# Weight parts of the first up unit made early and kept in DRAM, residual work in halves between the w_ple blocks, sums of squares on VectorE

## The chip, the cores and the metric

The kernel runs on one core of a Trainium2 chip. The metric is the device time of the whole launch in microseconds. Before the change three runs took 2024.33 to 2029.08 us, median 2027.07.

## The reference

One layer of a streaming encoder on 1056 tokens (1024 of a prompt, 32 of a sample), width 1024, all in float32. The attention and recurrence branches are mixed to `mix`; what matters here starts there:

```python
x = x + _rms_norm(mix @ w_out, g_post_mix)          # x1

hf = _rms_norm(x, g_pre_ffn)
a, u = jnp.split(hf @ w_up, 2, axis=-1)             # w_up: 1024 x 5632
...
ffn = (jax.nn.gelu(ac, approximate=True) * u) @ w_down
x = x + _rms_norm(ffn, g_post_ffn)
...
x = x + (pe @ w_ple) * jax.nn.sigmoid(x @ w_ple_gate)   # w_ple: 256 x 1024
```

## The kernel before

Activations lie with features on partitions and tokens on the free axis. From w_out on, the tokens stand in four groups of 264 (`H`), two to a pair. Every float32 product is made of three matmuls on float32r parts: a value is cast to a high part on ScalarE (`S.copy`, L182 and L1424 for weights, L1366 for activations) and the low part is the difference, made on VectorE (L185, L1425, L1367). `product` issues high x high, high x low and low x high (L201 to L203). A weight column block is loaded by SP into one of two `wr` buffers, and its two parts take two of eight `wb` buffers; `next_w` keeps the parts of two further blocks ahead.

The stages around the change, in the order of the program:

- **out**, two pairs (loop over `p`), each over eight columns `c` of w_out: one block of 24 matmuls of 128x264 for each of the pair's two groups, into one of six PSUM banks `mm`. `z_out` scales the bank into `z[g]` and squares it on ScalarE (L1281, L1283, L1286) and adds the squares on VectorE (L1287).
- During pair 1, for groups 0 and 1: `pair_norm(0)` (sums over partitions by one-column matmuls against `ones`, L1307; a reciprocal root on VectorE, L1318 and L212 to L218; then row scales spread over partitions by small matmuls, L302, and copied to `rbT`, L304), `x1_part` (product with the row scale, L1335, addition of x, L1336, store to `x1_d` by POOL, L1337, gain on ScalarE, L1339), `x1_squares` (L1345 to L1352) for the second norm, and `build_ops(0)`, which makes from z the seven operands of a Strassen-like 2x2 product, each cast (L1366) and differenced (L1367), with five more subtractions and additions (L1370, L1371, L1374, L1378) between.
- **w_ple blocks**: `ple_product(g)` for four groups of eight blocks of 6 matmuls. ScalarE copies each bank to a tile `ple` (L1401; three tiles of four columns), POOL stores it (L1403). Between the groups stand, for groups 2 and 3: `pair_norm(1)`, `x1_part(2)`, `x1_part(3)`, and `build_ops(1)`.
- **up units**, 22 of them. A unit multiplies seven weight parts with seven operands (L1582 to L1584) into banks X, Y and Z (the same PSUM as the six `mm` banks). `unit_raw` loads the unit's 2 x 512 KB of w_up by SP (L1413); `unit_parts` makes the seven parts, with four additions between (L1431 to L1433, L1438); `prepare(n)` runs it three parts ahead of the use. Unit 0 runs pair 0 first and then pair 1, so that pair 1's operands have time to be made; `after` evicts the banks (L1593 to L1611), and a bank's next group waits for that. Later units run both pairs at once.
- In unit 0, `last_ops` squares x1 of groups 2 and 3 on VectorE (L1551) and takes the last steps of `build_ops(1)`; `x1_sums` sums each group's squares over features by 3 x 8 x 2 one-column matmuls, 48 trace rows a group (L1307), then `pair_norm` makes the second row scale.

The order of the instructions on each engine is set by the framework's scheduler from the program's order, except where `behind(engine)` pins what follows behind the last instruction of that engine. Each engine runs its own list in order, and so do SP and POOL with the transfers that they issue; a transfer whose wait isn't over holds those behind it.

```python
def behind(*engines):
    st = ExitStack()
    for e in engines:
        ins = next(i for i in reversed(nc.cur_bb.bb.instructions) if i.engine == e.engine)
        st.enter_context(tc.issue_after(ins))
    return st
```

Of the kernel before, what the change touches and what calls it, by code (L numbers as in the profile page):

```python
# [59 lines left out]
def layer_kernel(  # L60
# [65 lines left out]
    act_d = [dp.tile([P, T], F32, name=f"act_d{f}") for f in range(NF)]  # L126

# [1181 lines left out]
    def pair_norm(p, scale, t=None):  # L1309
# [15 lines left out]
        if sums:  # L1325
            rows()
        return rows

    def x1_part(g):

        rb = rbT[:, H * g:H * g + H]
        for i in range(2):
            zz = z[g][:, 4 * i:4 * i + 4, :].bitcast(F32)
            x = x1q[g][i]
            V.tensor_tensor(zz, zz, rb.unsqueeze(1).to_broadcast([P, 4, H]), op=ALU.mult)  # L1335
            V.tensor_tensor(x[:], x[:], zz, op=ALU.add)  # L1336
            gdma(x1_d[:, 4 * i:4 * i + 4, H * g:H * g + H], x[:])  # L1337
            for k in range(4):
                S.mul(z[g][:, 4 * i + k, :].bitcast(F32), x[:, k, :], g_ffn[:, 4 * i + k:4 * i + k + 1])  # L1339

    def x1_squares(g):

        for i in range(2):
# [6 lines left out]
            else:  # L1350
                V.tensor_tensor(x[:, 0, :], x[:, 0, :], x[:, 1, :], op=ALU.add)
                V.tensor_tensor(sqz[g][:], sqz[g][:], x[:, 0, :], op=ALU.add)  # L1352

# [39 lines left out]
    def ple_product(g):  # L1393
        xs = pT.pop(g)
        for c in range(8):
# [6 lines left out]
            if c % 4 == 3:  # L1402
                gdma(ple_d[:, c - 3:c + 1, H * g:H * g + H], t[:])  # L1403

# [11 lines left out]
    def unit_parts(u):  # L1416

        f1, f2 = raw_w.pop(u)
        s1 = wp.tile([P, 4, P], F32, tag="wb", name=nm("sa"), bufs=8)[:]
        a11, a12, a21, a22 = f1[:, 0:4, :], f1[:, 4:8, :], f2[:, 0:4, :], f2[:, 4:8, :]  # L1420

        def parts(src):
            t = wp.tile([P, 2, 4, P], F32R, tag="wb", name=nm("wt"), bufs=8)
            S.copy(t[:, 0], src)  # L1424
            V.tensor_tensor(t[:, 1], src, t[:, 0].bitcast(F32), op=ALU.subtract)  # L1425
            ready_w.append(t)
# [3 lines left out]
        parts(a11)  # L1430
# [4 lines left out]
        parts(a11)  # L1435
        yield
        parts(a12)
        adder.tensor_tensor(a12, a12, a11, op=ALU.add)  # L1438
        yield
        parts(a21)  # L1440
        yield
        parts(s1)
        yield
        parts(a22)
        yield
        parts(a12)
        yield

    AHEAD = 3
    n_parts, gens = [0], {}  # L1450

    def prepare(n):

        while n_parts[0] < min(n + 1, 7 * NF):
            u, i = divmod(n_parts[0], 7)
            if i == 0:
                if u not in raw_w:
                    unit_raw(u)
                gens[u] = unit_parts(u)
# [52 lines left out]
    next(op1)  # L1512
    next(op1)
    prepare(2)
    ple_product(3)

# [41 lines left out]

    def x1_sums(g):
        if g == 2:  # L1560
            x1_t.append(tr_bank())
        with behind(E):
            sums88(x1_t[0], g, [x1q[g][k // 4][:, k % 4, :] for k in range(KT)])

    def up_unit(u):
# [294 lines left out]
```

## Time and profile before

| | |
|---|---|
| three runs | 2029.08, 2027.07, 2024.33 us; median 2027.07 |
| the profiled execution | 2029.94 us, span from first to last instruction 2028.2 us |
| mean granted TensorE clock | 0.995 |
| busy share: PE, DVE, ACT, POOL | 99%, 71%, 47%, 11% |
| out, pair 0 / pair 1 | 1065.0 to 1111.4 / 1111.4 to 1163.9 us |
| w_ple blocks | 1163.9 to 1197.1 us |
| up unit 0 / unit 1 from | 1197.1 / 1236.2 us |

PE is TensorE's matmuls, PEld its weight loads, DVE is VectorE, ACT ScalarE, POOL GpSimd. Times in rows are us from the span's start unless marked ns. A row of the timeline has start, duration, engine, line, operation, tiles, count and, in brackets, how long the engine stood idle before it and what ended that. A row of a table by stretches has length, busy time (count of instructions) of each engine, the granted clock (1.00 is full), the busy share of the 16 DMA engines and GB/s. A row of grouped instructions has count, busy time, mean ns of one, idle time before them and what ended it. A DMA row has count, KB each and the median from issue to landing, where the trace has it. Some matmul records can be missing. Line numbers are those of the kernel before, except where a run's own are named.

### The profile page before, as it was taken

The page shows a single profiled execution, that of the slowest core. Times are in us where ns is not written, and L with a number is a line of the kernel's source. Part 1 is how long each engine was busy: PE and PEld are TensorE (multiplying, and loading weights), DVE is VectorE, ACT ScalarE, POOL GpSimd, SP SyncE. Part 2 cuts the span into 40 slices and gives each one's busy share as a digit, 9 for nine tenths or more (in the row PEclk, how much of TensorE's full clock was granted, in tenths as well). Part 3 has the DMA queues.
Part 4 walks back from the last instruction along what each step waited for, and adds up shares of the span by engine and source line. Part 5 has one row for each costly group of instructions (what it writes and reads, how often), then busy time and mean ns, then how long its engine had stood idle before and what let it go on. Part 6 is the DMA issues. An engine that isn't in the chain of part 4 may idle for free.

```text
span 2028.2 us, 37446 instructions
## 1 busy us (share of the span) xinstructions
PE 1999.8 (99%) x14366; PEld 1970.6 (97%) x14366; DVE 1441.1 (71%) x3194; ACT 960.0 (47%) x2177; POOL 219.3 (11%) x307
## 2 busy tenths in 40 slices
PE   8999999999999999999999989999999999999998
PEld 6999999999999999999999989999999999999998
DVE  6778788688888888553553877888888884655552
ACT  6555556556666666441224753333333343444432
POOL 2001110000000000002000112333333310000000
PEclk9999999999999999999999998999999999999999
DMA  8322321411111111486653561222222245655542
GB/s 255 104 64 93 103 74 53 154 42 57 57 46 47 44 46 53 138 250 204 204 152 108 159 200 53 86 74 85 74 82 77 79 144 193 219 179 181 165 128 83
DMA packets 247640, 233.79 MB, mean 115 GB/s; under 512 B 13013, under 2 KB 218344, under 8 KB 247461
## 3 DMA queue, kind: packets, MB, share of 16 engines
q1 hardware_dynamic: 240501, 209.15, 33.3%
q0 software_dynamic: 6880, 22.17, 3.1%
q8 instruction: 113, 1.85, 0.4%
q14 instruction: 66, 0.54, 0.1%
q10 hardware_dynamic: 80, 0.07, 0.0%
HBM read 171.79 MB, written 59.55 MB: 114 GB/s over the span
## 4 chain that ended last, share of the span: by engine, by line
PE 88%; DVE 6%; issue 2%; DMA 2%; ACT 1%; POOL 0%; SPq 0%; ACTq 0%; DVEq 0%; POOLq 0%
PE mm L201 13%; PE mm L202 13%; PE mm L203 13%; PE st L1584 7%; PE st L1583 7%; PE st L1582 7%; PE G L841 2%; PE Y L838 2%; PE G L840 2%; PE G L838 2%; PE Y L841 2%; PE Y L840 2%; PE tr L470 1%; PE X L838 1%; PE so L1032 1%
## 5 line engine op out<-in xcount | busy, mean ns | idle before, releaser
L1582 PE MATMUL st<-op,wt 128*128 128x264 f32 x1232 | 351.2, 285 | 2.5 <-ACT ple L1401 2.5
L1584 PE MATMUL st<-op,wt 128*128 128x264 f32 x1232 | 352.6, 286 | 0.0
L1583 PE MATMUL st<-op,wt 128*128 128x264 f32 x1232 | 350.5, 285 | 0.0
L185 DVE TENSOR_TENSOR wl<-wr,wh 128x1024 fp32r<-128x1024 f32 x134 | 164.1, 1224 | 144.9 <-ACT wh L182 137.8
L1582 PEld LDWEIGHTS st<-op,wt 128*128 128x128 f32 x1232 | 234.0, 190 | 2.8 <-ACT ple L1401 2.8
L1583 PEld LDWEIGHTS st<-op,wt 128*128 128x128 f32 x1232 | 234.1, 190 | 0.0
L1584 PEld LDWEIGHTS st<-op,wt 128*128 128x128 f32 x1232 | 233.6, 190 | 0.0
L182 ACT CAST wh<-wr 128x1024 fp32r<-128x1024 f32 x115 | 120.7, 1050 | 213.9 <-PE mm L202 161.3
L201 PE MATMUL mm<-ac,wh 128*128 128x352 f32 x528 | 171.0, 324 | 0.9 <-DVE Sp L1611 0.9
L1424 ACT CAST wt<-wu 128x512 fp32r<-128x512 f32 x132 | 81.4, 620 | 190.7 <-POOL ab L1568 93.3
L203 PE MATMUL mm<-ac,wl 128*128 128x352 f32 x528 | 169.9, 322 | 0.0
L202 PE MATMUL mm<-ac,wh 128*128 128x352 f32 x528 | 169.5, 321 | 0.0
L201 PE MATMUL mm<-La,wh 128*128 128x384 f32 (+1 forms) x504 | 166.9, 332 | 0.0
L202 PE MATMUL mm<-Lb,wh 128*128 128x384 f32 (+1 forms) x504 | 163.2, 324 | 0.0
L203 PE MATMUL mm<-La,wl 128*128 128x384 f32 (+1 forms) x504 | 162.8, 323 | 0.0
L203 PE MATMUL mm<-Ra,wl 128*128 128x264 f32 x512 | 145.3, 284 | 1.3 <-DVE wl L185 1.3
L201 PE MATMUL mm<-Ra,wh 128*128 128x264 f32 x512 | 145.6, 285 | 0.0
L202 PE MATMUL mm<-Rb,wh 128*128 128x264 f32 x512 | 145.1, 284 | 0.0
L1425 DVE TENSOR_TENSOR wt<-wu,wt 128x512 fp32r<-128x512 f32 x132 | 106.8, 810 | 37.5 <-ACT wt L1424 37.3
L454 ACT ACTIVATE sc<-sc,st 128x257 f32<-128x257 f32 (+1 forms) x144 | 69.6, 485 | 84.6 <-DVE st L449 81.0
L201 PEld LDWEIGHTS mm<-ac,wh 128*128 128x128 f32 x528 | 99.1, 188 | 1.1 <-DVE Sp L1611 1.1
L202 PEld LDWEIGHTS mm<-ac,wh 128*128 128x128 f32 x528 | 99.7, 189 | 0.0
(461 smaller groups left out, 5734.1 us busy)
## 6 DMA issues: line engine op xcount, KB each, us to landing
wr<-in_w_down_dram SPq DMA_DIRECT2D x66, 512.0 KB
wu<-in_w_up_dram SPq DMA_DIRECT2D x44, 512.0 KB
wu<-in_w_in_dram SPq DMA_DIRECT2D x32, 512.0 KB
wr<-in_w_in_dram SPq DMA_DIRECT2D x26, 512.0 KB
ac<-act_d SPq DMA_DIRECT2D x66, 176.0 KB
act_d<-Up SPq DMA_DIRECT2D x21, 528.0 KB
wr<-in_w_out_dram SPq DMA_DIRECT2D x16, 512.0 KB
ya_d<-ya SPq DMA_DIRECT2D x8, 528.0 KB
```

Of the source, the lines that this page charges most:

```text
L182: S.copy(hi[:], raw[:])
L185: V.tensor_tensor(lo[:], raw[:], hi[:].bitcast(F32), op=ALU.subtract)
L201: E.matmul(ps, wh, a, start=first and n == 0, stop=False)
L202: E.matmul(ps, wh, b, start=False, stop=False)
L203: E.matmul(ps, wl, a, start=False, stop=last and n == len(ks) - 1)
L838: E.matmul(o, wh, x[0][k], start=first and k == 0, stop=False, skip_group_check=True)
L840: E.matmul(o, wh, x[1][k], start=False, stop=False, skip_group_check=True)
L1424: S.copy(t[:, 0], src)
L1425: V.tensor_tensor(t[:, 1], src, t[:, 0].bitcast(F32), op=ALU.subtract)
L1582: E.matmul(o, wh, xh, start=first and k == 0, stop=False, skip_group_check=True)
L1583: E.matmul(o, wh, xl, start=False, stop=False, skip_group_check=True)
L1584: E.matmul(o, wl, xh, start=False, stop=k == 3, skip_group_check=True)
```

## The change

- `early_parts` is new and runs one step after each block of pair 0 of out. It loads unit 0's raw w_up blocks and w_ple into pages that w_br_b's operands have left, makes unit 0's seven parts and w_ple's two high and two low parts in three slots of 512 KB, and POOL stores each of these eleven pieces in DRAM (`pw_d`). The additions between the parts stay on VectorE.
- w_ple leaves the plan of `next_w`. At c = 5 of pair 1 `load_ple` loads its four parts by SP; `load_part(0)` to `(3)` are placed ahead of the w_ple blocks, parts 4 to 6 in the first three steps of unit 0, where unit 1's raw load stands too. `prepare` starts with unit 1 (`n_parts = [7]`), in the second pass of unit 0, five parts ahead.
- In the w_ple blocks the pieces of work are placed at block numbers (`beside`): the row scales pinned behind block 3, `x1_sum` for quarters of x1 at 10, 13, 17, 20, `x1_gain` by pairs of columns three and four blocks later and pinned behind ScalarE's last instruction, steps of `build_ops(1)` at 25, 27, 30, squares of group 2 at 28, 29. The scheduler may still issue earlier what isn't pinned.
- Squares of groups 2 and 3 move from VectorE to ScalarE (`x1_square`), and `x1_add` sums the eight feature columns of squares on VectorE to one, so that the sum over partitions takes 3 one-column matmuls a group instead of 24 (each shown as two trace rows). They are issued once, behind the last step of unit 0's first pass.
- The load of x for group 0 moves from ahead of pair 0 to its column 6.

```diff
-    plan += [rows_cols(w_out, 0, c * P, P, KT) for c in (*range(8), *range(5))]
-    plan += [rows_cols(w_ple, 0, c * 512, 512, 2) for c in range(2)]
-    plan += [rows_cols(w_out, 0, c * P, P, KT) for c in range(5, 8)]
+    plan += [rows_cols(w_out, 0, c * P, P, KT) for c in (*range(8), *range(8))]
...
+    def x1_square(g, i):
+        x = x1q[g][i]
+        S.activation(x, x, AF.Square)
+
+    def x1_add(g):
+        a, b = x1q[g]
+        V.tensor_tensor(a, a, b, op=ALU.add)
+        V.tensor_tensor(a[:, 0:2, :], a[:, 0:2, :], a[:, 2:4, :], op=ALU.add)
+        sqz[g] = fo.tile([P, H], F32, tag=f"sqz{g}", name=nm("sq1"))
+        V.tensor_tensor(sqz[g][:], a[:, 0, :], a[:, 1, :], op=ALU.add)
...
-    def unit_parts(u):
+    def unit_parts(u, s1, place, out):
...
+    def early_parts():
+        rw = page(lq, 4, [P, 2, KT, P], "rw")
+        rs_ = page(lq, 5, [P, 2, 2, 512], "rs")
+        bufs = [page(lq, 6 + i, [P, 2, 2, 4, P], "pw") for i in range(2)]
+        raw_w[0] = [rw[:, i].bitcast(F32) for i in range(2)]
+        for i in range(2):
+            dma(raw_w[0][i], rows_cols(w_up, 0, DFF * i, P, KT)[0])
+        for i in range(2):
+            dma(rs_[:, i].bitcast(F32), rows_cols(w_ple, 0, 512 * i, 512, 2)[0])
+        place = [bufs[0][:, 0], bufs[0][:, 1], bufs[1][:, 0]]
+        def store(i, t):
+            gdma(pw_d[i][:], t.rearrange("p a k c -> p (a k c)").bitcast(F32))
+        yield from unit_parts(0, bufs[1][:, 1, 0].bitcast(F32), lambda i: place[i % 3], store)
+        for i in range(2):
+            src = rs_[:, i].rearrange("p k c -> p (k c)")
+            hi, lo = (place[(7 + 2 * i + a) % 3].rearrange("p a k c -> p (a k c)") for a in range(2))
+            S.copy(hi, src.bitcast(F32))
+            gdma(pw_d[7 + 2 * i][:], hi.bitcast(F32))
+            V.tensor_tensor(lo, src.bitcast(F32), hi.bitcast(F32), op=ALU.subtract)
+            gdma(pw_d[8 + 2 * i][:], lo.bitcast(F32))
+            yield
+    def load_ple():
+        for i in range(2):
+            ts = [wp.tile([P, 2, 512], F32R, tag="wb", name=nm("wq"), bufs=8) for _ in range(2)]
+            for a in range(2):
+                dma(ts[a][:].rearrange("p k c -> p (k c)").bitcast(F32), pw_d[7 + 2 * i + a][:])
+            ple_w.append(ts)
+    def load_part(i):
+        t = part_tile()
+        dma(t[:].rearrange("p a k c -> p (a k c)").bitcast(F32), pw_d[i][:])
+        ready_w.append(t)
...
-    x_load(0)
+    early = early_parts()
     for p in range(2):
         for c in range(8):
             if p and c == 5:
-                ple_w.extend((next_w(), next_w()))
-            w = next_w(4 if p and c in (3, 4) else 2)
-            if p and c == 7:
-                unit_raw(0)
+                load_ple()
+            w = next_w(2)
             for g in (2 * p, 2 * p + 1):
                 z_out(c, g, block(w, ALL, Ra[g], Rb[g], KS, H))
+                if p == 0 and (c, g) != (0, 0):
+                    next(early, None)
             if p == 0:
+                if c == 6:
+                    x_load(0)
                 continue
...
-    prepare(0)
-    pair_norm(1, 0.25 / D)
-    ple_product(0)
-    p_load(2)
-    x1_part(2)
-    ple_product(1)
-    p_load(3)
-    x1_part(3)
-    op1 = build_ops(1)
-    next(op1)
-    prepare(1)
-    ple_product(2)
-    next(op1)
-    next(op1)
-    prepare(2)
-    ple_product(3)
+    for i in range(4):
+        load_part(i)
+    rows = pair_norm(1, 0.25 / D, late=True)
+    op1 = build_ops(1)
+    def behind_s(f, *a):
+        with behind(S):
+            f(*a)
+    beside = {3: [lambda: pinned(rows, E)], 7: [lambda: p_load(2)], 15: [lambda: p_load(3)]}
+    for n, (g, i) in enumerate(((2, 0), (2, 1), (3, 0), (3, 1))):
+        m = (10, 13, 17, 20)[n]
+        beside.setdefault(m, []).append(lambda g=g, i=i: x1_sum(g, i))
+        for h in range(2):
+            beside.setdefault(m + 3 + h, []).append(
+                lambda g=g, i=i, h=h: behind_s(x1_gain, g, i, (2 * h, 2 * h + 1)))
+    for m in (25, 27, 30):
+        beside.setdefault(m, []).append(lambda: next(op1))
+    for i in range(2):
+        beside.setdefault(28 + i, []).append(lambda i=i: x1_square(2, i))
+    for g in range(4):
+        ple_product(g, beside)
...
     def last_ops(n):
-        if n in (1, 4):
-            for i in range(2):
-                x = x1q[2 + n // 4][i]
-                V.tensor_tensor(x, x, x, op=ALU.mult)
-        if n in (3, 6):
+        if n == 0:
+            unit_raw(1)
+        if n < 3:
+            load_part(4 + n)
+        if n < 2:
+            x1_square(3, n)
+        if n in (0, 3):
+            x1_add(2 + n // 3)
             next(op1)
         if n == 6:
-            x1_sums(2)
+            with behind(E):
+                x1_t.append(pair_norm(1, 1.0 / D, late=True))
...
-                elif ps == (0,):
-                    prepare(min(n + AHEAD, 6))
-                else:
-                    prepare(n + AHEAD)
+                elif ps == (1,):
+                    prepare(n + AHEAD + 2)
```

More of the change, by code (lines that the diff above doesn't have):

```diff
@@ L126, in layer_kernel @@
     act_d = [dp.tile([P, T], F32, name=f"act_d{f}") for f in range(NF)]
+    pw_d = [dp.tile([P, 1024], F32, name=f"pw_d{i}") for i in range(11)]
     def ltile(part, g):
@@ L1307, in sums88, with pair_norm @@
                 E.matmul(o, q[:, 88 * i:88 * i + 88], ones[:], start=k == 0, stop=k == len(sq) - 1)
-    def pair_norm(p, scale, t=None):
+    def pair_norm(p, scale, t=None, late=False):
         sums = t is None
@@ L1324, in rows, with x1_sum, x1_gain @@
                 norm_rows(rs[:, 3 * h:3 * h + 3], T88, rbT[:, o:o + H])
-        if sums:
+        if sums and not late:
             rows()
         return rows
+    def x1_sum(g, i):
+        rb = rbT[:, H * g:H * g + H]
+        zz = z[g][:, 4 * i:4 * i + 4, :].bitcast(F32)
+        x = x1q[g][i]
+        V.tensor_tensor(zz, zz, rb.unsqueeze(1).to_broadcast([P, 4, H]), op=ALU.mult)
+        V.tensor_tensor(x[:], x[:], zz, op=ALU.add)
+        gdma(x1_d[:, 4 * i:4 * i + 4, H * g:H * g + H], x[:])
+    def x1_gain(g, i, ks=range(4)):
+        for k in ks:
+            S.mul(z[g][:, 4 * i + k, :].bitcast(F32), x1q[g][i][:, k, :], g_ffn[:, 4 * i + k:4 * i + k + 1])
     def x1_part(g):
-        rb = rbT[:, H * g:H * g + H]
         for i in range(2):
[L1333 to L1339, printed above, removed]
+            x1_sum(g, i)
+            x1_gain(g, i)
     def x1_squares(g):
@@ L1391, in p_load, with ple_product @@
         pT[g] = xs
-    def ple_product(g):
+    def ple_product(g, beside):
         xs = pT.pop(g)
@@ L1403, in ple_product @@
                 gdma(ple_d[:, c - 3:c + 1, H * g:H * g + H], t[:])
+            for f in beside.pop(8 * g + c, ()):
+                f()
     raw_w, ready_w = {}, []
```

43 lines of the change are left out of this document (17 added, 26 removed).

## The prediction

> **What bounds the kernel now.** First the page's head and its busy shares.
>
> ```profile
> span 2028.2 us, 37446 instructions
> ...
> PE 1999.8 (99%) x14366; PEld 1970.6 (97%) x14366; DVE 1441.1 (71%) x3194; ACT 960.0 (47%) x2177; POOL 219.3 (11%) x307
> ```
>
> TensorE is the bound, and 99% busy says nothing of how fast it is. So I cut the span at the change: pair 0 of out, pair 1, the w_ple blocks, the first up unit, and 40 us of later units as the norm (columns: PE, PEld, DVE, ACT, POOL busy, granted clock, DMA share, GB/s).
>
> ```profile
> 1065.00:1111.40 46.40, 46.40 (x387) 46.40 (x386) 16.14 (x26) 19.51 (x39) 0.00 (x0) 1.00 0.39 115
> 1111.40:1163.90 52.50, 50.95 (x426) 50.36 (x425) 43.79 (x72) 36.79 (x69) 6.46 (x9) 1.00 0.46 143
> 1163.90:1197.10 33.20, 27.55 (x226) 26.73 (x224) 27.44 (x44) 24.54 (x61) 8.56 (x12) 1.00 0.74 243
> 1197.10:1236.20 39.10, 39.09 (x277) 38.94 (x278) 20.25 (x46) 9.87 (x18) 0.95 (x3) 0.74 0.26 71
> 1236.20:1276.20 40.00, 40.00 (x333) 40.00 (x332) 35.64 (x51) 15.91 (x22) 15.73 (x10) 1.00 0.27 84
> ```
>
> The norm is 40.00/333 = 0.120 us a matmul. Three losses show: holes of 33.20 - 27.55 = 5.7 us in the w_ple blocks, a clock of 0.74 in the first unit, and holes of 1.6 in pair 1. PE's timeline names the holes, by the idle time in brackets:
>
> ```profile
> 1144.12 0.39 PE L203 MATMUL mm<-Ra,wl 128*128 128x264 f32 x1 [0.57 <-DVE wl L185]
> ...
> 1157.87 0.39 PE L203 MATMUL mm<-Ra,wl 128*128 128x264 f32 x1 [0.77 <-DVE wl L185]
> ...
> 1186.24 0.39 PE L201 MATMUL mm<-pc,wh 128*128 128x264 f32 x1 [2.51 <-ACT ple L1401]
> 1192.84 0.39 PE L201 MATMUL mm<-pc,wh 128*128 128x264 f32 x1 [0.49 <-ACT ple L1401]
> 1197.11 0.39 PE L1582 MATMUL st<-op,wt 128*128 128x264 f32 x1 [2.54 <-ACT ple L1401]
> ```
>
> The last three are PSUM banks that ScalarE has not yet copied out. What it did instead:
>
> ```profile
> 1177.51 3.37 ACT L1339 ACTIVATE z<-x,gvec 128x264 f32<-128x264 f32 x8
> 1180.78 0.91 ACT L1401 COPY ple<-mm 128x264 f32<-128x264 f32 x3
> 1181.57 1.10 ACT L1366 CAST op<-z 128x1056 fp32r<-128x1056 f32 x1
> 1182.55 3.37 ACT L1339 ACTIVATE z<-x,gvec 128x264 f32<-128x264 f32 x8
> 1185.81 2.02 ACT L1401 COPY ple<-mm 128x264 f32<-128x264 f32 x7
> 1187.69 1.12 ACT L1366 CAST op<-z 128x1056 fp32r<-128x1056 f32 x1
> ...
> 1195.14 0.66 ACT L1401 COPY ple<-mm 128x264 f32<-128x264 f32 x2 [1.52 <-DMA ple_d<-ple]
> ```
>
> Eight gains in a row, twice, then casts. Spacings: a gain 3.37/8 = 0.42, a copy 2.02/7 = 0.29, a cast 1182.55 - 1181.57 = 0.98. In the first unit PE has no hole, but 96 one-column matmuls, and a halved clock:
>
> ```profile
> 1208.96 4.53 PE L1307 MATMUL tr<-ones,x 128*88 128x1 f32 x48
> 1216.14 7.10 PE L1307 MATMUL tr<-ones,x 128*88 128x1 f32 x48
> ...
> 1233.06 1.54 PE L302 MATMUL tr<-ident,nr 88*128 88x88 f32 x12
> ```
>
> ```profile
> 1192.00:1196.00 4.00, 2.08 (x15) 1.00 0.90 301
> 1196.00:1200.00 4.00, 2.89 (x17) 0.78 1.06 261
> ...
> 1208.00:1212.00 4.00, 4.00 (x49) 0.98 0.00 0
> 1212.00:1216.00 4.00, 4.00 (x23) 0.50 0.00 0
> ...
> 1224.00:1228.00 4.00, 4.00 (x20) 0.50 0.00 0
> 1228.00:1232.00 4.00, 4.00 (x31) 0.88 0.00 0
> ```
>
> The clock falls after the 2.54 us hole and again at the end of the first 48 sums, and is back only at about 1229. Lost in the unit: 0.26 x 39.10 = 10.2 us, of which 7.10 - 4.53 = 2.6 lie in the second sums.
>
> **The change, part by part.** Prices not yet shown:
>
> ```profile
> L182 ACT CAST wh<-wr 128x1024 fp32r<-128x1024 f32 x15 | 15.8, 1053 | 22.7 <-PE mm L202 21.7 <-DMA wr<-in_w_out_dram 1.1
> L1424 ACT CAST wt<-wu 128x512 fp32r<-128x512 f32 x13 | 7.9, 627 | 4.4 <-PE st L1584 2.9 <-DVE rst L216 0.6 <-DVE wt L1425 0.6
> L1425 DVE TENSOR_TENSOR wt<-wu,wt 128x512 fp32r<-128x512 f32 x11 | 7.6, 688 | 0.5 <-ACT wt L1424 0.4
> L1345 ACT ACTIVATE x<-x 128x1056 f32<-128x1056 f32 x4 | 4.3, 1098 | 0.1
> ```
>
> ```profile
> 1169.28 0.16 DVE L1318 TENSOR_SCALAR nv<-tr 88x6 f32<-88x6 f32 x1 [1.01 <-PE tr L1307]
> ...
> 1171.96 0.17 DVE L218 SCALAR_TENSOR_TENSOR nr<-rst,nr 128x6 f32<-128x6 f32 x1
> 1173.59 2.43 DVE L1335 TENSOR_TENSOR z<-z,rbT 128x1056 f32<-128x1056 f32 x2 [1.47 <-ACT rbT L304]
> ```
>
> ```profile
> x_d<-x POOLq DMA_DIRECT2D x8, 528.0 KB, 6.3
> ple_d<-ple POOLq DMA_DIRECT2D x8, 528.0 KB, 5.9
> ...
> h_d<-La POOLq DMA_DIRECT2D x4, 192.0 KB, 2.6
> ```
>
> *1. Parts made in pair 0.* ScalarE gets 7 x 0.63 + 2 x 1.05 = 6.5 us, VectorE 11 x 0.69 + 2 x 1.22 = 10.0 (a w_ple subtraction is the shape of wl, L185, as its cast is that of L182): 26.0 and 26.2 of 46.4 us, so both have room. POOL issues 11 stores, SP four more loads. The stores go through three slots, and a cast that waits for its slot holds z_out and the next w_out cast behind it on ScalarE. The store's time is not in the trace: 2.6 us at 192 KB below, 6.3 at 528 KB above; I take 6.3, the nearer size. One use of a slot is 0.63 + 0.69 + 0.75 issue + 6.3 = 8.4 us, so 11 uses take 11 x 8.4/3 = 31 us of the 46.4. Cover: six banks of 24 x 0.120 = 2.9 us each let z_out be 17 us late; a w_out cast runs about two columns, 11 us, ahead of its use. Price 0.
>
> *2. Pair 1* loses the two w_ple splits (2 x 1.22 on VectorE). The c = 5 split takes their place, so the 0.57 hole goes. The c = 7 split stays behind the same x4 additions while PE arrives earlier: its hole of 0.77 becomes some 1.5. Net 0.
>
> *3. The w_ple blocks*, with T = 0 at 1163.9 and the orders and waits that the built program has. PE: 32 blocks of 6 x 0.120 = 0.72, so 23.1 us, and the norm's small matmuls. The sums stand behind block 1; the rsqrt chain on VectorE takes 1171.96 + 0.17 - 1169.28 = 2.85 us before, with one foreign subtraction of 0.69 in it that goes: some 2.5 now. The rows are pinned behind block 3, so PE gets there 0.6 us too early (hole 1). The row scale is in SBUF at 5.7. VectorE needs four products and four additions of 2.43/2 = 1.2 us: the x1 quarters are there at 9.3, 10.5, 14.0 and 15.2, while before the first gain ran at 1177.51, 13.6. ScalarE has nothing but copies until block 13 (12.7 us). From there to the copy of block 30 stand 16 gains x 0.42 = 6.7, 17 copies x 0.29 = 4.9, and two casts and two squares at 1.0 = 4: 15.6 us, so 28.3. In between the gains stand in pairs, and the six banks hold PE's lead: it ends its blocks, unhindered, at 25.2. Its first up matmul (bank X) waits for the copy of block 30: hole 2, 28.4 - 25.2 = 3.2. Bank Y waits for the last copy, which stands behind two more casts, at 28.3 + 2.0 + 0.3 = 30.6, and X's 12 matmuls are done at 29.8: hole 3, 0.8. So the loss at the change of phase shrinks but stays: with x1 ready early, ScalarE's own work is late next. Start of up 28.4, before 1197.1 - 1163.9 = 33.2.
>
> *4. First unit.* Parts 0 to 3 are loaded when the last w_out columns are used; the loads of the per-layer inputs of groups 2 and 3 stand behind them on SP and are not needed before block 16. Parts 4 to 6 go by SP when w_ple's last use is over; behind them on SP stand only unit 1's raw weights, not used for some 10 us. Part 4 has from 22.3 to 32 to land; the trace has no landing of an SP load, from 2.6 (192 KB) to 6.3 (528 KB) by POOL's: covered at both; a landing of 12 us would cost 2. ScalarE copies s1c behind the last copy, a cast and two squares, at 34.0, and X's second group, part 2, may not start before: hole 4, 0.8. VectorE: the first cast of op1 is ready at 12.7 + 6.7 + 12 x 0.29 + 1.0 = 23.9, and behind it stand ten operations of 1.17 to 1.2, one of half size, then Y's eviction: 36.5, with PE there at 35.4 (hole 5, 1.1). The next evictions stand between more such operations: holes of 0.2, 0.7 and, in the second pass, 0.8. The row sums of x1 squares move to VectorE and leave 6 of 96 matmuls: 4.53 + 7.10 - 6 x 0.1 = 11.0 us less, and the array is no longer fed one column at a time.
>
> *Sum.* After: 360 matmuls x 0.120 = 43.2, small matmuls of two norms 3 (two times 1.54 at most for the rows), holes 0.6 + 3.2 + 0.8 + 0.8 + 1.1 + 0.2 + 0.7 + 0.8 = 8.2: 54.4 us from 1163.9 to unit 1, against 1236.2 - 1163.9 = 72.3, so -17.9. As terms: sums -11.0, clock -(10.2 - 2.6) = -7.6, holes 8.2 - 5.7 = +2.5, the rest rounding of these bounds. The later units have the same work in the same order: 0. I hold back 2 us for transfers (DMA share 0.74 in the blocks, and 2 MB of parts more) and for the clock: **-16**. The profiled execution took 2029.94 (span 2028.2) and would take 2013.9; the three runs' median is 2027.07, 2.9 lower, so 2011.1.
>
> Hole 2 is longer than the one that halved the clock at 1197. If it does so for some 4 us, the slow matmuls fill holes 3 and 4, which are there anyway; hence no term of its own.
>
> [...]
>
> **Rivals.**
> - *The gate stays shut* through the first unit, as it did for 17 us from 1212: for, the seven small holes after the long one; against, the sums that kept PE's array empty are gone. Price 17 x 0.5 = 8.5 less the 3 us of holes it fills: -10.5, 2017. [...]
> - *Transfers pace the blocks*: the ple tiles are three, each filled in 2.9 us, and its store, behind x1_d stores on POOL, lands in 5.9; with parts loads beside, at 9 us a ring turn is 2.9 + 0.75 + 9 = 12.7, 4.2 a tile for 2.9: 8 x 1.3 = 10 us, half of it hidden in ScalarE's lag. -11, 2016. For: ScalarE's 1.52 wait at 1195.14.
> - *It doesn't free PE*: the six sums stand behind VectorE's whole chain. If that starts 10 us later (x loads late), PE's time goes from sums to a hole: -4 to 0, 2025.
> - *Slower*: pair 0's slots. If a store took 21 us, 11 uses would take 11 x 23/3 = 84 us; less 46.4 and 17 of banks, PE would stand 20 us and the total be 2031. It decides from there (about 14 us a store gives the first PE hole). Against: 6.3 us, and a share of 0.39.
>
> **How the numbers follow.** About 0.2%, 4 us, is what can be told from no change. Forecast (-12 to -21) 0.62; gate 0.12; transfers 0.12; sums only moved 0.07; slots 0.07. Faster by over 0.2%: 0.62 + 0.12 + 0.12 = 0.86, within 0.07, slower 0.07. The range takes the forecast's own, 2006 to 2015, the two middle rivals up to 2021, and below 1 us for a store time at its low bound: 2005 to 2021.
>
> **What would show it.** Pair 0: PE 46.4 of 46.4 still, ACT near 26, DVE near 26. Blocks: one hole of 2 to 4 us ahead of the first st matmul, none of 2.5 inside. First unit: L1307 six times, under 1 us; clock 0.85 or more; holes on VectorE of about 1 us each; unit 1 at about 1218. Wrong if w_out or part loads end PE's waits, if the clock stays at 0.5 past 1205, or if pair 0 has PE holes.

## The result, and the profile after

The changed kernel takes 2018.86 us (median of 13 runs, 2015.46 to 2023.93) against 2027.43 us for the kernel before (13 runs, 2020.92 to 2033.74): a ratio of 0.9963, 95% interval 0.9951 to 0.9976. It is faster, by 7.5 to 8.6 us where 16 were forecast. The profiled execution took 2021.98 us, span 2020.3, against 2029.94 and 2028.2. Line numbers here are those of each kernel's own file; the changed kernel's sums are L1306, its w_ple copies L1420, its up matmuls L1647 to L1649.

Busy times by stretch of the changed kernel (columns as before): out pair 0, pair 1, w_ple blocks, unit 0, 40 us of later units.

```profile
1070.20:1116.60 46.40, 46.40 (x386) 46.40 (x385) 25.25 (x39) 24.52 (x48) 7.40 (x13) 1.00 0.89 291
1116.60:1170.30 53.70, 51.78 (x434) 51.21 (x433) 41.50 (x74) 35.08 (x68) 6.81 (x9) 1.00 0.62 197
1170.30:1201.90 31.60, 26.41 (x219) 25.84 (x217) 16.19 (x25) 22.05 (x56) 8.28 (x11) 0.99 0.88 297
1201.90:1228.90 27.00, 25.94 (x193) 25.58 (x194) 25.19 (x51) 12.99 (x20) 0.95 (x3) 0.89 0.29 90
1228.90:1268.90 40.00, 39.19 (x324) 38.98 (x323) 32.32 (x49) 15.38 (x21) 14.81 (x10) 1.00 0.25 81
```

Pair 0 takes 46.40 us of full TensorE as before. The first unit fell from 39.10 to 27.00. The blocks fell from 33.20 to 31.60 only, where 28.4 was forecast, and a hole came into the later units. Out itself began at 1070.2 instead of 1065.0, before anything that was changed. The holes on TensorE's timeline:

```profile
1161.28 0.63 PE L1306 MATMUL tr<-ones,sq 128*88 128x1 f32 x6 [1.58 <-DVE sq L1359]
...
1192.00 0.36 PE L200 MATMUL mm<-pc,wq 128*128 128x264 f32 x1 [1.13 <-DMA pc<-pc_d]
1201.89 0.59 PE L1647 MATMUL st<-op,wt 128*128 128x264 f32 x1 [3.79 <-ACT ple L1420]
1209.99 0.39 PE L1647 MATMUL st<-op,wt 128*128 128x264 f32 x1 [1.06 <-ACT Sp L1658]
1244.39 0.39 PE L1647 MATMUL st<-op,wt 128*128 128x264 f32 x1 [0.81 <-DVE Sp L1665]
```

The hole of 3.79 us ahead of unit 0 is the forecast's hole 2 (3.2). The table by stretches of four us around it, where the granted clock stands ahead of the DMA share:

```profile
1198.00:1202.00 4.00, 0.21 (x2) 0.11 (x1) 3.97 (x4) 4.00 (x8) 0.75 (x1) 0.87 1.00 317
1202.00:1206.00 4.00, 4.00 (x18) 4.00 (x19) 4.00 (x5) 4.00 (x6) 0.75 (x1) 0.50 1.04 342
1206.00:1210.00 4.00, 2.94 (x18) 2.73 (x17) 4.00 (x5) 1.37 (x3) 0.00 (x0) 0.77 0.87 251
```

The clock halves again: 18 matmuls in four us instead of 33. ScalarE's timeline around that hole:

```profile
1183.88 0.93 ACT L1340 ACTIVATE z<-x,gvec 128x264 f32<-128x264 f32 x2
...
1195.08 0.38 ACT L1420 COPY ple<-mm 128x264 f32<-128x264 f32 x1 [2.62 <-PE mm L201]
...
1196.44 1.08 ACT L1385 CAST op<-z 128x1056 fp32r<-128x1056 f32 x1
...
1199.20 1.12 ACT L1363 ACTIVATE x<-x 128x1056 f32<-128x1056 f32 x1
1200.18 0.40 ACT L1420 COPY ple<-mm 128x264 f32<-128x264 f32 x1
1200.44 1.13 ACT L1363 ACTIVATE x<-x 128x1056 f32<-128x1056 f32 x1
1201.42 0.41 ACT L1420 COPY ple<-mm 128x264 f32<-128x264 f32 x1
```

VectorE's one long wait in the blocks, by its timeline:

```profile
1197.55 1.26 DVE L1386 TENSOR_TENSOR op<-z,op 128x1056 fp32r<-128x1056 f32 x1 [11.50 <-ACT op L1385]
```

The copy that ends at 1201.83 releases unit 0; two squares stand ahead of it, and earlier a wait of 2.62 us. The gains begin only at 1183.88, 13.6 us behind the start of the blocks, and VectorE, which had x1 ready, stood idle for 11.50 us until op1's first cast. The sums, last, on TensorE's timeline:

```profile
1217.62 1.03 PE L1306 MATMUL tr<-ones,sq 128*88 128x1 f32 x12
```

### The profile page after: what moved, and what is told of

Same layout as the page of the kernel before. It is cut to its first block, busy times and chain, and to the rows that moved or that the text cites. A ratio compares the mean times of both kernels' runs of the same rounds, so it can differ in the third digit from the quotient of the medians.

```text
span 2020.3 us, 37338 instructions
## 1 busy us (share of the span) xinstructions
PE 1988.2 (98%) x14282; PEld 1957.6 (97%) x14282; DVE 1440.4 (71%) x3196; ACT 964.0 (48%) x2181; POOL 224.6 (11%) x318
## 4 chain that ended last, share of the span: by engine, by line
PE 87%; DVE 7%; issue 2%; DMA 2%; ACT 2%; SPq 0%; POOL 0%; ACTq 0%; DVEq 0%; POOLq 0%
PE mm L200 13%; PE mm L201 13%; PE mm L202 13%; PE st L1649 7%; PE st L1648 7%; PE st L1647 7%; PE G L840 2%; PE Y L837 2%; PE G L839 2%; PE G L837 2%; PE Y L840 2%; PE Y L839 2%; PE tr L469 1%; PE X L837 1%; PE so L1031 1%
## 5 line engine op out<-in xcount | busy, mean ns | idle before, releaser
L1647 PE MATMUL st<-op,wt 128*128 128x264 f32 x1232 | 349.8, 284 | 5.7 <-ACT ple L1420 3.8
L1649 PE MATMUL st<-op,wt 128*128 128x264 f32 x1232 | 350.9, 285 | 0.0
L184 DVE TENSOR_TENSOR wl<-wr,wh 128x1024 fp32r<-128x1024 f32 x132 | 161.6, 1224 | 128.5 <-ACT wh L181 118.0
L1647 PEld LDWEIGHTS st<-op,wt 128*128 128x128 f32 x1232 | 232.6, 189 | 6.4 <-ACT ple L1420 4.0
L1649 PEld LDWEIGHTS st<-op,wt 128*128 128x128 f32 x1232 | 232.1, 188 | 0.0
L202 PE MATMUL mm<-Ra,wl 128*128 128x264 f32 x512 | 145.0, 283 | 0.0
L1445 DVE TENSOR_TENSOR wt<-wu,wt 128x512 fp32r<-128x512 f32 x126 | 102.2, 811 | 39.8 <-ACT wt L1444 39.8
```

Source lines behind the costliest of these rows:

```text
L184: V.tensor_tensor(lo[:], raw[:], hi[:].bitcast(F32), op=ALU.subtract)
L202: E.matmul(ps, wl, a, start=False, stop=last and n == len(ks) - 1)
L1647: E.matmul(o, wh, xh, start=first and k == 0, stop=False, skip_group_check=True)
L1649: E.matmul(o, wl, xh, start=False, stop=k == 3, skip_group_check=True)
```

## Experiments

The profiled executions of two kernels can be compared only over the stretch that the change touches: out began anywhere from 1063.3 to 1070.2 us in the executions below. So beside each ratio stands the time from the first matmul of out to the first of unit 1 in the profiled execution (a row of the table by stretches over just that), and the mean granted clock of all runs of the kernel.

| kernel | ratio to before, 95% interval | out to unit 1, us | mean clock |
|---|---|---|---|
| before; again | 1.0003 (0.9991 to 1.0014) | 171.2; 168.8 | 0.994 |
| changed; again | 0.9963; 0.9959 (0.9945 to 0.9974) | 158.7; 161.4 | 0.997 |
| sums_alone | 0.9955 (0.9939 to 0.9971) | 156.8 | 0.997 |
| old_sums | 1.0018 (1.0007 to 1.0028) | 171.3 | 0.994 |
| fill | 0.9969 (0.9956 to 0.9982) | 161.3 | 0.997 |
| squares_late | 0.9961 (0.9946 to 0.9975) | 161.7 | 0.997 |
| no_store2 | 0.9967 (0.9953 to 0.9981) | 161.6 | 0.997 |
| halves_only | 0.9967 (0.9955 to 0.9979) | 162.3 | 0.997 |
| early_only; again | 0.9938 (0.9915 to 0.996); 0.9924 (0.9905 to 0.9944) | 155.4; 155.3 | 0.998 |
| halves_soon | 0.995 (0.9934 to 0.9966) | 159.3 | 0.997 |
| early_norm | 0.991 (0.9889 to 0.9931) | 153.7 | 0.999 |

### Both kernels again

> The kernel before, unchanged, for a second profile and for the granted clock of each of its runs. Theory: the clock gate is drawn anew in each execution, so that before loses about 10 us to it in one execution and 5 in another, and its first 880 us, which the change doesn't touch, move by up to 5 us from run to run. Rival: the loss is the same in each execution (clock of 0.995 in all, the first matmul of out at 1065.0 again), and then the 5.3 us by which the changed kernel came later to out belong to the change.

> The changed kernel, unchanged. Theory: out begins at 1065 or at 1070, by the draw of the gate at 40 us, and from the start of out to unit 1 it takes 158.7 again, within 2. Rival: out begins at 1070 in each execution of it. Ratio 0.996, as before.

Out began at 1069.9 in the second execution of before and at 1065.7 in the second of the changed kernel, the other way round: those 5 us are no part of the change. The rest of the changed kernel's theory missed: 161.4 us came back, not 158.7 within 2. The granted clock of before's runs went from 0.991 to 0.998, and a lower clock goes with a longer time (2034.95 us at 0.991, 2022.71 to 2023.43 at 0.998). The theory of the draw fits: from out to unit 1 before had a clock of 0.94 in one execution and 0.96 in the other. One number of the forecast falls with it: the loss of 10.2 us to the clock in unit 0 was that of one execution. The long sums on the timeline of before in its second execution:

```profile
1214.52 3.85 PE L1307 MATMUL tr<-ones,x 128*88 128x1 f32 x48
1219.82 4.46 PE L1307 MATMUL tr<-ones,x 128*88 128x1 f32 x30
1223.84 3.07 PE L1307 MATMUL tr<-ones,x 128*88 128x1 f32 x20
```

The whole stretch from out to unit 1 in before's first and second execution, at clocks of 0.94 and 0.96, and in the changed kernel's first:

```profile
1064.98:1236.19 171.21, 164.00 (x1311) 162.43 (x1309) 107.61 (x185) 90.71 (x186) 15.97 (x23) 0.94 0.45 138
1069.91:1238.67 168.76, 161.22 (x1310) 159.43 (x1309) 107.46 (x185) 90.89 (x186) 15.97 (x23) 0.96 0.46 140
...
1070.24:1228.89 158.65, 150.48 (x1226) 148.98 (x1225) 108.12 (x188) 94.63 (x191) 23.45 (x36) 0.98 0.69 226
```

48 rows take 3.85 us at the full clock, not 4.53. The changed kernel's second execution has the same holes on TensorE's timeline, two of them clearly longer; its hole in pair 1, 1.67 us, halved the clock there for 3.4 us from 1158.7, which the first execution's 1.58 did not:

```profile
1190.21 0.36 PE L200 MATMUL mm<-pc,wq 128*128 128x264 f32 x1 [2.26 <-DMA pc<-pc_d]
1200.09 0.59 PE L1647 MATMUL st<-op,wt 128*128 128x264 f32 x1 [3.77 <-ACT ple L1420]
1208.19 0.39 PE L1647 MATMUL st<-op,wt 128*128 128x264 f32 x1 [2.40 <-ACT Sp L1658]
```

### One part alone, and one part undone: the sums

In the kernel before, VectorE adds up each group's squares, and one column is summed over the partitions:

```diff
                 V.tensor_tensor(x, x, x, op=ALU.mult)
+            x1_add(2 + n // 4)
...
-            sums88(x1_t[0], g, [x1q[g][k // 4][:, k % 4, :] for k in range(KT)])
+            sums88(x1_t[0], g, [sqz[g]])
```

> The kernel before with one part of the change alone: the eight columns of squares are added on VectorE, so that the sums over partitions take 6 one-column matmuls instead of 48; parts and residual stay where they were. Theory (the sums are the gain): start of out to unit 1 falls from 171.2 by 10.5 for the sums, and by up to 4 for the clock that no longer falls in them, less 2 for VectorE's additions: 160, a ratio of 0.995, as the whole change. Rival (the early parts and the halves carry half of it): 166 or more, 0.998.

In the changed kernel, the other way round:

```diff
-            x1_add(2 + n // 3)
...
-                x1_t.append(pair_norm(1, 1.0 / D, late=True))
+                t = tr_bank()
+                for g in (2, 3):
+                    sums88(t, g, [x1q[g][k // 4][:, k % 4, :] for k in range(KT)])
+                x1_t.append(pair_norm(1, 1.0 / D, t))
```

> The changed kernel with the 48 one-column matmuls back in place of VectorE's additions, all at one place behind unit 0's first pass. Theory: the sums take 3.6 us each at a full clock, 7.2 - 0.9 = 6.4 more, and the clock falls in them, 2 to 5 more: 8 to 11 us over the changed kernel, so about the time before (0.999 to 1.002). Rival (VectorE's additions cost as much as they save): within 3 us of the changed kernel.

The sums alone give 0.9955, as much as the whole change, and a shorter stretch than it. Its row of the table by stretches:

```profile
1069.18:1225.98 156.80, 148.62 (x1227) 146.57 (x1225) 109.89 (x189) 90.13 (x186) 15.98 (x23) 1.00 0.49 151
```

And its hole ahead of unit 0, after which the clock stayed at 1.00:

```profile
1201.08 0.39 PE L1590 MATMUL st<-op,wt 128*128 128x264 f32 x1 [2.56 <-ACT ple L1401]
```

With the old sums the changed kernel loses all that it had won. On its timeline the sums stand in one piece:

```profile
1213.27 9.79 PE L1306 MATMUL tr<-ones,x 128*88 128x1 f32 x96
```

Its table by stretches shows the clock fall behind them:

```profile
1214.00:1218.00 4.00, 4.00 (x54) 4.00 (x53) 0.13 (x1) 0.84 (x1) 0.00 (x0) 1.00 0.00 0
1218.00:1222.00 4.00, 4.00 (x31) 4.00 (x31) 0.00 (x0) 0.23 (x1) 0.00 (x0) 0.53 0.02 4
1222.00:1226.00 4.00, 4.00 (x22) 4.00 (x22) 2.76 (x7) 1.12 (x2) 0.00 (x0) 0.50 0.00 0
```

TensorE was busy by its records in all of 1214 to 1218, with one-column matmuls, and the clock halved at 1218.3 for 10.2 us. All three executions with 96 rows of sums show such a fall, within or just behind the sums; in the others the sums of unit 0 (12 rows) have none.

### Three attempts on the hole ahead of unit 0

Matmuls into a free bank, in the place of the hole:

```diff
+    def fill(n):
+        t = tr_bank()
+        with behind(E):
+            for k in range(n):
+                E.matmul(t[:, 0:H], ready_w[0][:, 0, k % 4, :], ops[0][0][:, 0, k % 4, :],
+                         start=k == 0, stop=k == n - 1)
+
+    fill(26)
```

> The changed kernel with 26 matmuls more, into a bank that nobody reads, between the last w_ple block and the first matmul of unit 0, where TensorE stood idle for 3.79 us: 26 x 0.12 = 3.1 us of them. Theory (the idle time shuts the clock gate): the clock stays at 1.00 through unit 0, and unit 1 starts 2.5 to 3 us earlier than in the changed kernel. Rival (the gate follows something else, or the slow matmuls only fill waits): the same time, or up to 0.5 us longer.

Group 2's squares behind the copies:

```diff
-    for i in range(2):
-        beside.setdefault(28 + i, []).append(lambda i=i: x1_square(2, i))
...
-        if n < 2:
-            x1_square(3, n)
+        if n < 4:
+            with behind(S):
+                x1_square(2 + n // 2, n % 2)
+        if n in (1, 3):
+            x1_add(2 + n // 3)
         if n in (0, 3):
-            x1_add(2 + n // 3)
             next(op1)
```

> The changed kernel with the two squares of group 2 taken out of the w_ple blocks: all four squares are pinned behind ScalarE's last w_ple copies, in unit 0. Theory (ScalarE's list sets the hole): the copy of block 30 ends two squares of 0.98 earlier, the hole ahead of unit 0 falls from 3.79 to 1.8, the gate stays open (a hole of 2.51 left it open), and unit 1 starts 2 us earlier by the hole and up to 2.7 by the clock. Rival (the stores' landing sets it): hole and time as in the changed kernel.

The stores of x1 of groups 2 and 3 left out of the blocks:

```diff
-        gdma(x1_d[:, 4 * i:4 * i + 4, H * g:H * g + H], x[:])
+        if g < 2:
+            gdma(x1_d[:, 4 * i:4 * i + 4, H * g:H * g + H], x[:])
```

> The changed kernel without the stores of x1 of groups 2 and 3 during the w_ple blocks (x itself is copied into their place in the first stage, so the mixed part is missing from two groups of the result). 4 x 528 KB less beside the blocks. Theory (transfers delay the ple stores, for which ScalarE waited 2.62 us at 1195.08, and the load of the per-layer inputs, for which TensorE waited 1.13 us at 1192.00): both waits go, the hole ahead of unit 0 falls to 1.5, and unit 1 starts 3 us earlier, 5 with the clock. Rival (ScalarE's own list is as long): less than 1 us.

None of the three came out as its theory had it: 161.3, 161.7 and 161.6 us, no better than the changed kernel's 158.7 and 161.4. The holes on TensorE's timeline of fill:

```profile
1186.78 0.36 PE L200 MATMUL mm<-pc,wq 128*128 128x264 f32 x1 [2.00 <-DMA pc<-pc_d]
1204.72 0.39 PE L1656 MATMUL st<-op,wt 128*128 128x264 f32 x1 [2.67 <-ACT Sp L1667]
```

Those of squares_late:

```profile
1193.21 0.39 PE L1647 MATMUL st<-op,wt 128*128 128x264 f32 x1 [1.83 <-ACT ple L1420]
1202.99 0.59 PE L1647 MATMUL st<-op,wt 128*128 128x264 f32 x1 [5.14 <-ACT Sp L1658]
```

Those of no_store2:

```profile
1158.10 0.63 PE L1306 MATMUL tr<-ones,sq 128*88 128x1 f32 x6 [4.16 <-DVE sq L1360]
...
1197.52 0.39 PE L1651 MATMUL st<-op,wt 128*128 128x264 f32 x1 [2.42 <-ACT ple L1421]
...
1205.63 0.39 PE L1651 MATMUL st<-op,wt 128*128 128x264 f32 x1 [2.94 <-ACT Sp L1662]
```

With the fill, unit 0 started at a full clock, but the next hole grew from 1.06 to 2.67 and halved the clock there, at 1205.3; another of 2.00 had halved it at 1188.2. With the squares late, the hole fell to 1.83, as forecast, and 5.14 us came back ten us later: ScalarE's copy stood behind a cast that waited for unit 1's weights, by its timeline:

```profile
1202.04 0.62 ACT L1444 CAST wt<-wu 128x512 fp32r<-128x512 f32 x1 [2.88 <-DMA wu<-in_w_up_dram]
```

Without the stores, TensorE's wait for the per-layer inputs went, and so did ScalarE's wait among the w_ple copies, 2.62 us in the changed kernel. That one is for the store of the w_ple tile whose buffer the copy takes: in fill ScalarE's timeline names it.

```profile
1189.81 0.38 ACT L1420 COPY ple<-mm 128x264 f32<-128x264 f32 x1 [3.47 <-DMA ple_d<-ple]
```

From the first w_ple matmul to the first of unit 0 no_store2 took 28.4 us, the changed kernel 31.1 and 32.2. So the transfers do delay the blocks, by some 3 us. Most of that was lost again: the wait of 2.94 in unit 0 halved the clock there, and the longer wait in pair 1 (4.16) did so before the blocks.

In all three, what is saved ahead of unit 0 returns as a wait inside it. In fill and no_store2 it is a ScalarE copy that waits for a subtraction of op1 on VectorE. The chain of gains, casts and differences of op1 stands behind that wait as well as behind the hole; only no_store2 moved it forward, by 2.7 us to 24.1 behind the first w_ple matmul. In squares_late it is the load above. That the chain is what holds unit 0 is argued from these waits; these three runs don't show it by themselves.

### Early parts or halves

The changed kernel with the parts made where they were before:

```diff
-    early = early_parts()
+    x_load(0)
...
-    n_parts, gens = [7], {}
+    n_parts, gens = [0], {}
...
-    for i in range(4):
-        load_part(i)
+    prepare(0)
```

> The changed kernel without its early parts: unit 0's parts and w_ple's are made where they were before the change, and nothing goes through DRAM; the residual in halves and the sums on VectorE stay. From the start of out to unit 1 the traces have 171.2 and 168.8 us for before, 156.8 for the sums alone, 158.7 and 161.4 for the whole change. Theory (the early parts' loads delay the per-layer inputs and the stores, and the halves are worth nothing): 155 to 158, TensorE's wait for the per-layer inputs gone, a ratio of 0.994 to 0.996. Rival (the halves cost, not the transfers): 159 to 162.

And with the residual and the squares where they were before:

```diff
-    rows = pair_norm(1, 0.25 / D, late=True)
...
-    for g in range(4):
-        ple_product(g, beside)
+    pair_norm(1, 0.25 / D)
+    ple_product(0, {})
+    p_load(2)
+    x1_part(2)
+    ple_product(1, {})
+    p_load(3)
+    x1_part(3)
+    op1 = build_ops(1)
+    next(op1)
+    ple_product(2, {})
+    next(op1)
+    next(op1)
+    ple_product(3, {})
...
-            x1_square(3, n)
+                V.tensor_tensor(x, x, x, op=ALU.mult)
```

> The changed kernel with the residual work and the squares where they were before the change (gains eight in a row on ScalarE, squares of groups 2 and 3 on VectorE); early parts in DRAM and the sums on VectorE stay. Theory (transfers): a wait of 1 to 2.5 us for the per-layer inputs again, and 159 to 163 us from the start of out to unit 1. Rival (the halves cost): 155 to 158.

My theory fell and its rival stood, twice: the halves cost, and the early parts don't. One clause of the theory held: TensorE's wait for the per-layer inputs is gone in halves_only; in early_only it is 0.66 us, less than expected. "Halves" stands here for the residual in pieces and the squares on ScalarE together; no run takes these two apart. halves_only, from out to unit 1:

```profile
1067.80:1230.08 162.28, 153.02 (x1226) 150.69 (x1225) 107.18 (x188) 95.06 (x191) 15.97 (x23) 0.97 0.46 146
```

Its two longest holes:

```profile
1200.04 0.59 PE L1644 MATMUL st<-op,wt 128*128 128x264 f32 x1 [4.30 <-ACT ple L1422]
1208.14 0.39 PE L1644 MATMUL st<-op,wt 128*128 128x264 f32 x1 [2.02 <-ACT Sp L1655]
```

early_only, from out to unit 1, at a clock of 1.00:

```profile
1065.79:1221.15 155.36, 148.49 (x1227) 146.59 (x1225) 112.68 (x192) 90.41 (x187) 23.38 (x36) 1.00 0.71 231
```

And its two longest holes:

```profile
1157.25 0.63 PE L1306 MATMUL tr<-ones,sq 128*88 128x1 f32 x6 [2.00 <-DVE sq L1359]
...
1195.83 0.39 PE L1641 MATMUL st<-op,wt 128*128 128x264 f32 x1 [1.89 <-ACT ple L1420]
```

With the sums on VectorE in all of them, four kernels make a square: neither 156.8, early parts alone 155.4 and 155.3, halves alone 162.3, both 158.7 and 161.4. The hole ahead of unit 0 goes the same way: 2.56, 1.89, 4.30, 3.79; and the clock fell there only in the two that have the halves. Two executions of one kernel differ by up to 2.7 us in this stretch, so the 3 to 6 us of the halves stand clear of that and the 1.5 us of the early parts don't. The ratios agree for the halves: the interval of early_again, 0.9905 to 0.9944, lies below both of the changed kernel's, though that of early_only, 0.9915 to 0.996, overlaps them. ScalarE's timeline in early_only:

```profile
1176.21 3.36 ACT L1340 ACTIVATE z<-x,gvec 128x264 f32<-128x264 f32 x8
1179.48 2.02 ACT L1420 COPY ple<-mm 128x264 f32<-128x264 f32 x7
1181.37 3.38 ACT L1340 ACTIVATE z<-x,gvec 128x264 f32<-128x264 f32 x8
1184.63 1.08 ACT L1385 CAST op<-z 128x1056 fp32r<-128x1056 f32 x1
```

Eight gains in a row, the very thing that made a hole of 2.51 in before, but begun 10 us behind the start of the blocks (1166.3), and op1's first cast 18.3 behind it; in the changed kernel 13.6 and 26.1.

### Halves begun sooner, a norm placed later, and the best again

```diff
-        m = (10, 13, 17, 20)[n]
+        m = (5, 8, 12, 15)[n]
...
-    for m in (25, 27, 30):
+    for m in (20, 22, 25):
...
-        beside.setdefault(28 + i, []).append(lambda i=i: x1_square(2, i))
+        beside.setdefault(23 + i, []).append(lambda i=i: x1_square(2, i))
```

> The changed kernel with every piece of the residual five w_ple blocks earlier (sums behind blocks 5, 8, 12, 15, gains three and four blocks later, casts of op1 at 20, 22, 25, squares at 23, 24). In the changed kernel VectorE stood idle for 11.50 us ahead of op1's first difference, since the gains are pinned behind blocks 13 to 24, though x1 was there. Theory (that late start is what the halves cost): 5 x 0.72 = 3.6 us of the idle time go, the waits in unit 0 shrink, and from the start of out to unit 1 it takes 155 to 158 instead of 158.7 and 161.4; mean clock as in early_only, 0.998. Rival (the halves cost because ScalarE's four squares and pairs of gains stand among its copies, wherever they begin): 158 or more.

In early_only:

```diff
-            if c == 5:
-                pair_norm(0, 1.0 / D)
...
+            if c == 7:
+                pair_norm(0, 1.0 / D)
```

> early_only with the first pair's second norm (sums, row scales) two columns later in pair 1 of out. early_only has a hole of 2.00 us there, since its sums wait for VectorE's squares; that hole is in all kernels with early parts (1.6 to 2.0) and in none without (0.4 to 0.8). Theory (a place too early for VectorE's list): the hole goes and the stretch from out to unit 1 falls from 155.4 to 153.5. Rival (VectorE is late by itself, so the wait moves to a split of w_out or to the w_ple blocks): the same 155.

> early_only again, unchanged, for more runs on the chip that the others run on. If the early parts without the halves are the better kernel: a ratio of 0.993 to 0.995, below that of the sums alone (0.9955), mean clock 0.998, and 155 to 156 us from the start of out to unit 1. If its first six runs were a lucky draw of the gate: 0.9955 or more.

In halves_soon VectorE's wait fell by more than was expected:

```profile
1188.64 1.26 DVE L1386 TENSOR_TENSOR op<-z,op 128x1056 fp32r<-128x1056 f32 x1 [6.02 <-ACT op L1385]
```

The stretch took 159.3, of which 3.1 us are the excess of 31 matmuls at a halved clock. That is above the 155 to 158 of the theory, so by the stretch its rival stood. The ratio of 0.995 lies below the changed kernel's 0.9959 and 0.9963, but the intervals overlap, and the mean clock did not rise to 0.998. In this one execution the gain is behind pair 1: from the first w_ple matmul to unit 1 it took 56.7 us, the changed kernel 58.1 and 59.3, while a wait of 2.18 in pair 1 halved the clock there. The late start may be part of what the halves cost; the run doesn't show it. early_norm came out as its theory had it, from out to unit 1:

```profile
1064.91:1218.56 153.65, 147.98 (x1227) 146.38 (x1226) 112.08 (x191) 90.73 (x187) 23.41 (x36) 1.00 0.72 234
```

The 2.00 in pair 1 is down to 0.60, while the wait for the per-layer inputs grew from 0.66 to 1.55. With 2011.76 us (4 runs) against 2030.04 it has the lowest median of this study, but its interval overlaps that of early_again, which confirms early_only, at 0.9924.

## Why the prediction was right or wrong

The direction, the cause (the sums) and the new hole ahead of unit 0 were right; the forecast size was about double the measured one. That the median lies inside the range of 2005 to 2021 is no merit of the sum: its own range ended at 2015, and the upper part was there for two rivals. The stretch from out to unit 1, term by term, for two executions of each kernel:

| us | before | again | changed | again | mean difference | forecast |
|---|---|---|---|---|---|---|
| one-column sums | 14.0 | 13.3 | 3.5 | 3.5 | -10.1 | -11.0 |
| other matmuls, excess at half clock | 5.3 | 3.0 | 2.7 | 2.8 | -1.4 | -7.6 |
| holes | 7.2 | 7.5 | 8.2 | 10.7 | +2.1 | +2.5 |
| the rest | 144.7 | 145.0 | 144.3 | 144.4 | -0.5 | -1.8 |
| all | 171.2 | 168.8 | 158.7 | 161.4 | -10.0 | -17.9 |

The second line counts 53, 30, 27 and 28 matmuls of some 0.222 us in half-clock stretches, at 0.222 less 0.122 each. Behind it, unit 1 up to the down stage takes 427.3 in both executions of before and 428.4 in both of the changed kernel: +1.1, 0.81 of it the hole at 1244.39. -10.0 + 1.1 = -8.9 is what the medians show (-8.6 in both comparisons).

- **The step that failed** is "clock -(10.2 - 2.6) = -7.6": the term measures -1.4. Its first part is the loss in before. The 10.2 was one execution's. Of it, more than 2.6 lay inside the sums, which the term of -11.0 had already counted: 58 of before's rows ran at 0.147 us and not at 0.078, which is 4.0 us (48 rows, 3.3 us, in the second execution). That leaves 5.3 and 3.0 outside the sums, 4.2 on average, where 7.6 was taken. Its second part is the changed kernel, where the term had no loss: 2.7 and 2.8 us. Hole 2 halved the clock in both executions; in the second, about half of the 2.8 stands behind the hole of 1.67 in pair 1. In all, sums included, the clock gave some 5 where 10.2 was forecast. The mean clock of all runs says nearly the same: from 0.9940 (28 runs of before) to 0.9967 is 0.0027 x 2020 = 5.5 us.
- **"Hence no term of its own"**, the sentence that lets the slow matmuls fill holes, was not far off. From the first w_ple matmul to unit 1, holes and excess together are 8.9 and 10.0 us where the sum has 8.2. TensorE's wait for the per-layer inputs, 1.13 and 2.26, which the sum doesn't have, is in them.
- **The sums** as such were right: 84 trace rows fewer at 0.078 are 6.6 us at a full clock. Of the forecast's 11.0, 2.6 were put down to the clock; the other 8.4 came of taking 4.53 us for a full-clock price, though the clock fell within those rows too. sums_alone and old_sums show that this part is the whole gain.
- **The 1.8 us** that the forecast put down to rounding had no term behind it, and only 0.5 of it came; that the 2 us held back in the total made up for it is luck. It is no rounding: the sum has 43.2 + 3 = 46.2 us for the 360 matmuls and the small ones, and early_only, at a full clock all the way from the first w_ple matmul to unit 1, is busy for 49.9 with them. That is 3.7 us too little on the side of the changed kernel.

```profile
1166.73:1221.15 54.42, 49.89 (x405) 48.56 (x404) 45.93 (x79) 30.52 (x71) 9.21 (x14) 1.00 0.65 216
```

- **The parts in pair 0** at price 0: right. Pair 0 stays at 46.40, ScalarE at 24.5 and VectorE at 25.3 (26 each were forecast), and a store takes 5.0 us by the row of the DMA issues below, where 6.3 was taken. early_only even takes 1.5 us less than sums_alone, which is within the scatter.

```profile
pw_d<-pw POOLq DMA_DIRECT2D x11, 512.0 KB, 5.0
```

- **Pair 1** at net 0: holes of 0.57 and 0.77 gave way to one of 1.58, not at the c = 7 split but at the sums of the first pair's second norm. early_norm shows that a later place for them takes that hole away, for 1.6 us. In the changed kernel's second execution the hole (1.67) also halved the clock, for 3.4 us.
- **The blocks**: hole 2 of 3.2 came as 3.79 and 3.77; the copy of block 30 released unit 0 as forecast, but 31.5 us and not 28.4 behind the blocks' start. Of the 3.1 us between, TensorE's wait for the per-layer inputs is 1.13 (2.26 in the second execution), and ScalarE's wait for the store of a w_ple tile is 2.62 at 1195.08, though its row names a matmul that had long ended. Both go in no_store2, and unit 0 then starts 28.4 us behind the first w_ple matmul (31.1 in the changed kernel by that measure).
- **Unit 0**: hole 5 of 1.1 came as 1.06 and 2.40; holes 3 and 4 didn't come. That the slow matmuls took their place, as the forecast had it, fits, but no run shows it apart.
- **The rivals**: behind hole 2 the clock was at half for 6.8 and 3.4 us in the changed kernel's two executions, not through the unit. Transfers paced the blocks in part, for some 3 us by no_store2. The sums did not only move. The slots didn't hold pair 0.
- That halves would feed TensorE better was in the prediction only as its holes, and there rightly at a loss (+2.5). I didn't draw the consequence, that the change without them would be faster.

The prediction set hole 2, at 3.2 us, against the one of 2.54 that had halved the clock in before, and took some 4 us at half clock for the case that it did so again. The hole came as 3.79 and 3.77, and the clock did halve, for 6.8 and 3.4 us.

## What to carry to other kernels

A loss to the clock can differ from one execution to the next, as here in before (5.3 and 3.0 us outside the sums): take it from several executions, and take it out of the matmuls that a change removes before it is counted by itself. A hole that is closed in front of a chain can come back behind it, as in fill, unless the chain itself starts earlier; look for the engine that waits longest ahead of the chain (here VectorE, 11.50 us, and never over 0.84 in early_only), not only for the hole that TensorE shows. And a change of several parts deserves each part alone: here one part was the whole gain, one gave or cost too little to tell, and one cost 3 to 6 us.

## What the runs showed of the hardware

In the trace of before the granted clock was 0.50 for 3.4 us from 1198.2, behind the hole of 2.54, and for 17.1 us from 1211.9, within the sums; in that of the changed kernel for 6.8 us from 1201.0, near the end of the hole of 3.79. The fourteen profiled executions, from 1110 us to the end of unit 0, have these holes of over 1.6 us on TensorE's timeline:

| holes, us | a stretch at half clock followed | the clock stayed at 1.00 |
|---|---|---|
| 2.94 to 5.14 | 2.94 and 4.16 (no_store2), 2.96 (halves_soon), 3.73 (old_sums), 3.77 (changed, again), 3.79 (changed), 4.30 (halves_only), 5.14 (squares_late) | none |
| 1.67 to 2.67 | 1.67 (changed, again), 1.68 and 1.76 (before, again: one stretch, behind the second), 2.00 and 2.67 (fill), 2.02 (halves_only), 2.18 (halves_soon), 2.54 (before) | 1.74 and 2.11 (old_sums), 1.79 and 1.83 (squares_late), 1.86 and 1.90 (early_again), 1.89 and 2.00 (early_only), 2.04 (fill), 2.26 and 2.40 (changed, again), 2.42 (no_store2), 2.51 (before), 2.51 (before, again), 2.51 and 2.56 (sums_alone) |

In these executions half clock followed all eight holes of 2.94 us and more. From 1.67 to 2.67 it followed some and not others, and the length alone does not tell which: 2.51 did nothing in before and 2.54 did, while 2.56 did nothing in sums_alone.

The three executions with 96 rows of one-column sums also have half clock from within or just behind the sums, with no hole on TensorE's timeline in the 8 us before it: for 17.1 us in before, 10.2 in its second execution and in old_sums. That the fall comes of the sums is argued from these three and from the others, which have 12 rows of sums in unit 0 and no fall there.
